# Down projection of a SwiGLU feed-forward network: newest hidden tiles taken from SBUF, residual loads spread over the steps, the second pass begun with a kept tile

## The chip, the cores and the metric

The kernel runs on one core of a Trainium2 chip. A core has five engines that work at the same time, each through its own queue of instructions in a fixed order: PE (matrix multiplications), DVE (elementwise vector work), ACT (activations and casts), POOL (elementwise work as well) and SP, which here issues DMAs. They wait for each other by semaphores. The metric is the device time of one execution in microseconds (us); lower is better.

## The reference, cut to what matters

Two layers are computed for 1024 tokens of 1024 numbers. Each ends with a feed-forward network behind a residual and a layer norm:

```python
def swiglu_ffn(x, w_in, w_out):
    gate, up = jnp.split(x @ w_in, 2, axis=-1)
    return (jax.nn.silu(gate) * up) @ w_out

for layer in range(2):
    ...
    x = _layer_norm(ALPHA * x + mix, ln_mix_g[layer], ln_mix_b[layer])
    x = _layer_norm(ALPHA * x + swiglu_ffn(x, ffn_w_in[layer], ffn_w_out[layer]),
                    ln_ffn_g[layer], ln_ffn_b[layer])
```

The hidden size is 2816. All is float32. The change concerns the product with `w_out`, called the down projection here, its residual `ALPHA * x`, and the norm behind it.

## The kernel before

`ffn` runs once per layer. Its first part, `hidden(j)` for 22 tiles j of 128 hidden numbers, makes a tile `hf` of h (128 hidden numbers by 1024 tokens): DVE writes its first half at L695 and its second at L699, from `u2` (L697) after ACT's Silu (L698), and SP stores it to memory (`scr_h`, L700), since all 22 tiles of h with their splits would not fit in SBUF.

The second part is the down projection, `down(0)` and `down(1)`: a pass for each half of the 1024 output numbers. A pass has 22 steps, one per hidden tile. A step needs two operands in two parts each, a high part cast by ACT (L197) and a low part subtracted by DVE (L200), both from `split`: the tile of h read back from memory (`load_hidden`: `wraw` to `hh` and `hl`, 128x1024) and a block of `f_out` (`block`: `wraw` to the two halves of `wb`, 128x512 each). `raw_load` has three buffers (`N_RAW = 3`), and a next load waits until a split has freed one. `mm3` (L229 to L231) makes three matmuls for each of eight token tiles: high by high, high by low, low by high. So a step is 24 matmuls, into eight PSUM banks `pd`, one per token tile.

At the end of a pass DVE adds the bank of each token tile to the residual, `acc = ALPHA * acc + pd` (L722), and takes statistics of it (L723). `acc` are eight tiles of 128x1024, loaded in step 0 of `down(0)` (L735, all eight one after the other) and multiplied and shifted by the gain of the norm before (`ln_gain`, two instructions of POOL each, L352 and L353, with `g_row` and `b_row`).

The last six tiles of h (`KEEP = 6`) stay split in SBUF from the first pass to the second. In `down(1)` the first sixteen steps run as above; then the six kept tiles run with the token tile as the outer loop, so that a token tile is finished early and its norm can follow: `ln` in layer 0, `ln_out` in layer 1, which writes the result (L754 to L769). `ln_out` needs the last norm's `g_row` and `b_row`. They are loaded between the two calls of `down`, into the same two buffers (tag `row`) that the rows of `ln_gain` hold.

The order on each engine's queue is set by a scheduler that goes by data dependences and estimates of its own; `pace` gives it one more dependence, on the last matmul written so far, which orders the instruction and makes nothing wait on the chip.

## Time and profile before

| | us |
|---|---|
| median of 3 runs | 2683.41 |
| lowest and highest run | 2683.39, 2695.26 |
| the profiled execution | 2686.94 |
| its span | 2685.1 |
| PE busy | 2533.1 (94%) |
| DVE busy | 1672.4 (62%) |
| ACT busy | 1135.9 (42%) |
| POOL busy | 505.3 (19%) |

The span is the part of the execution that the profiler recorded; starts in the rows count from its beginning. The down projection of layer 0 begins at 775.40 us, that of layer 1 at 2402.41 us. In a row of a timeline the bracket at the end tells how long the engine had stood idle before, and whose work released it. PE is busy nearly all the time, so what is looked for are the stretches in which it isn't.

### The profile page before, as it was taken

Reading aid. Unit: us, or ns where it says so; the run is one execution under the profiler, and the core shown is the slowest. Engines: PE = TensorE matmul, PEld = TensorE weight load, DVE = VectorE, ACT = ScalarE, POOL = GpSimd, SP = SyncE. Lnnn points to the kernel's source line nnn. Section 1 sums busy time; section 2 is a strip of 40 time slices with the busy share of each in tenths; the row PEclk is TensorE's granted clock in tenths of the full one; section 3 lists DMA queues with packets and bytes.
Section 4 is the critical chain, followed back from the end, with each engine's and each line's share of the span. In section 5 each row is a group of like instructions: output and inputs, shape, how many; then the busy total and the mean of one; then the engine's idle time right before and its main releaser. Section 6 shows DMA issues by size and latency. Waiting matters only on the chain. (4 is left out here: it accounts for less than half of the span.)

```text
span 2685.1 us, 41451 instructions
## 1 busy us (share of the span) xinstructions
PE 2533.1 (94%) x16064; PEld 2018.1 (75%) x16064; DVE 1672.4 (62%) x2981; ACT 1135.9 (42%) x2192; POOL 505.3 (19%) x526
## 2 busy tenths in 40 slices
...
GB/s 143 124 25 114 107 85 88 86 77 81 79 160 199 135 99 95 168 153 177 203 165 101 92 95 88 69 48 131 67 102 102 79 79 86 79 130 183 177 106 63
DMA packets 258181, 297.89 MB, mean 111 GB/s; under 512 B 149952, under 2 KB 191040, under 8 KB 257984
## 3 DMA queue, kind: packets, MB, share of 16 engines
...
## 5 line engine op out<-in xcount | busy, mean ns | idle before, releaser
L641 PE MATMUL py<-xch,wb 128*128 128x512 f32 x1056 | 356.6, 400 | 4.4 <-DVE u L690 2.4
L229 PE MATMUL pd<-wb,hh 128*128 128x512 f32 x704 | 282.2, 401 | 21.9 <-ACT wb L197 14.2
L197 ACT CAST wb<-wraw 128x512 fp32r<-128x512 f32 x220 | 135.2, 619 | 376.8 <-PE py L641 173.9
L231 PE MATMUL pd<-wb,hl 128*128 128x512 f32 x704 | 281.9, 400 | 6.9 <-DVE hl L200 6.9
L230 PE MATMUL pd<-wb,hh 128*128 128x512 f32 x704 | 281.4, 400 | 1.5 <-DVE wb L200 1.5
L200 DVE TENSOR_TENSOR wb<-wraw,wb 128x512 fp32r<-128x512 f32 x220 | 161.0, 735 | 145.1 <-ACT wb L197 143.0
L641 PEld LDWEIGHTS py<-xch,wb 128*128 128x128 f32 x1056 | 200.3, 190 | 62.8 <-DVE u L690 15.7
L641 PE MATMUL pz<-xch,wb 128*128 128x512 f32 x704 | 233.4, 393 | 4.5 <-ACT xch L197 4.5
L641 PE MATMUL px<-xch,wb 128*128 128x512 f32 x704 | 233.9, 395 | 3.2 <-ACT p L652 3.2
L352 POOL TENSOR_TENSOR acc<-acc,g_row 128x1024 f32<-128x1024 f32 x24 | 62.4, 2605 | 845.3 <-DMA acc<-res 824.0
L197 ACT CAST wb<-sums 128x512 fp32r<-128x512 f32 x176 | 108.6, 621 | 257.1 <-PE pz L641 144.3
L641 PE MATMUL py<-xcl,wb 128*128 128x512 f32 x528 | 209.4, 397 | 1.6 <-DVE xcl L200 1.6
L200 DVE TENSOR_TENSOR wb<-sums,wb 128x512 fp32r<-128x512 f32 x176 | 123.2, 703 | 102.3 <-ACT wb L197 101.5
L200 DVE TENSOR_TENSOR hl<-wraw,hh 128x1024 fp32r<-128x1024 f32 x76 | 107.1, 1411 | 115.8 <-ACT hh L197 115.8
L229 PEld LDWEIGHTS pd<-wb,hh 128*128 128x128 f32 x704 | 135.7, 193 | 55.7 <-ACT wb L197 15.5
L231 PEld LDWEIGHTS pd<-wb,hl 128*128 128x128 f32 x704 | 135.0, 192 | 38.2 <-DVE hl L200 7.8
L1180 PEld LDWEIGHTS <-lt 128*128 128x128 f16 x1792 | 88.5, 103 | 97.1 <-issue 71.3
L230 PEld LDWEIGHTS pd<-wb,hh 128*128 128x128 f32 x704 | 135.2, 192 | 33.4 <-DVE wb L200 2.7
L641 PEld LDWEIGHTS pz<-xch,wb 128*128 128x128 f32 x704 | 132.5, 189 | 34.5 <-ACT xch L197 5.3
L641 PEld LDWEIGHTS px<-xch,wb 128*128 128x128 f32 x704 | 131.9, 188 | 34.9 <-ACT p L652 5.5
L269 POOL TENSOR_TENSOR rstd<-ve,mhalf 128x1 f32<-128x1 f32 x48 | 37.9, 792 | 627.0 <-DVE ve L267 590.9
L1180 PE MATMUL pX<-lt 128*128 128x64 f16 x1280 | 92.3, 201 | 63.1 <-DVE lt L1313 33.4
...
## 6 DMA issues: line engine op xcount, KB each, us to landing
wraw<-in_f_in_dram SPq DMA_DIRECT2D x96, 512.0 KB, 3.6
wraw<-scr_h SPq DMA_DIRECT2D x76, 512.0 KB, 3.9
scr_h<-hf SPq DMA_DIRECT2D x44, 512.0 KB, 2.6
...
res<-acc SPq DMA_DIRECT2D x16, 512.0 KB, 2.6
acc<-res SPq DMA_DIRECT2D x16, 512.0 KB, 6.7
wraw<-in_w_r_dram SPq DMA_DIRECT2D x16, 512.0 KB, 3.8
wraw<-in_w_k_dram SPq DMA_DIRECT2D x16, 512.0 KB, 4.2
```

Source lines behind the costliest of these rows:

```text
L197: nc.scalar.copy(hi, src)
L200: return (eng or nc.vector).tensor_tensor(lo, src, f(hi), op=ALU.subtract)
L229: nc.tensor.matmul(ps, ls(ah), rs(bh), start=start, stop=False)
L230: nc.tensor.matmul(ps, ls(ah), rs(bl), start=False, stop=False)
L231: c.last_mm = nc.tensor.matmul(ps, ls(al), rs(bh), start=False, stop=stop)
L269: c.last_pow = nc.gpsimd.tensor_tensor(r, ve, c.mhalf[:, 0:1], op=ALU.pow)
L352: c.nc.gpsimd.tensor_tensor(x, x, rows[0], op=ALU.mult)
L641: c.last_mm = nc.tensor.matmul(ps, a_[:, k * P:(k + 1) * P], b_[:, k % 2, :], start=start and k == i == 0, stop=False, skip_group_check=True)
L1180: keep(nc.tensor.matmul(*a, **k))
```

## The change

Five things are changed in the down projection.

1. The tiles of h are taken in another order: 20, 21, then 0 to 19. The last two, just made, are split from `hf` in SBUF (`fresh`) instead of being read back. They are stored for the second pass a little later, when their step is loaded.
2. A step's weight block is loaded and split ahead of its tile of h.
3. The eight `acc` are loaded one per step, in steps 4 to 11 (`ACC_AT = 4`), not all in step 0.
4. The last norm's rows are loaded in step 13 of the first pass, by an entry that `pace` puts there, not between the passes.
5. The second pass begins with a kept tile (19), then reads 20, 21, 0 to 13, and ends with the five kept tiles 14 to 18 in the loop over token tiles. The steps at positions 1 and 2 are loaded in the middle of the step before, and the low half of their weight is put behind that place (`late`).

```diff
--- before.py
+++ after.py
@@ -67,6 +67,7 @@
 LN_A = {3: (0,), 4: (1,), 5: (2,), 6: (3,)}
 JP = 4
 KEEP = 6
+ACC_AT = 4
 BANKS = "bbbaaacc"
 HP = 4
 CH = 64
@@ -163,9 +164,11 @@
                        bufs=dict(a=NB_A, b=NB_B, c=NB_C)[which])
 
 
-def bcast_row(c, row_ap, n, name):
+def bcast_row(c, row_ap, n, name, late=False):
     t = c.pool.tile([P, 1024], F32, name=name, tag="row", bufs=2)
-    c.nc.sync.dma_start(t[:, 0:n], row_ap[:, 0:n].to_broadcast([P, n]))
+    d = c.nc.sync.dma_start(t[:, 0:n], row_ap[:, 0:n].to_broadcast([P, n]))
+    if late:
+        pace(c, d)
     return t
 
 
@@ -353,8 +356,8 @@
     c.nc.gpsimd.tensor_tensor(x, x, rows[1], op=ALU.add)
 
 
-def ln_rows(c, name):
-    return bcast_row(c, c.row(name + "_g"), D, "g_row"), bcast_row(c, c.row(name + "_b"), D, "b_row")
+def ln_rows(c, name, late=False):
+    return [bcast_row(c, c.row(name + e), D, e[1] + "_row", late) for e in ("_g", "_b")]
 
 
 
@@ -627,11 +630,13 @@
 
     nc = c.nc
 
-    def block(src):
+    def block(src, late=False):
 
         t_ = c.pool.tile([P, 1024], F32R, name="wb", tag="w", bufs=N_W)
         hi, lo = t_[:, 0:512], t_[:, 512:1024]
-        split(c, hi, lo, src)
+        last = split(c, hi, lo, src)
+        if late:
+            pace(c, last)
         return hi, lo
 
     def prod(ps, w, name, start=False):
@@ -697,12 +702,15 @@
         nc.vector.tensor_tensor(u2, pz, u2, op=ALU.add)
         nc.scalar.activation(u2, u2, AF.Silu)
         nc.vector.tensor_tensor(hf[:, 512:1024], u3, u2, op=ALU.mult)
-        nc.sync.dma_start(hscr[j], hf)
-
-    acc, dest, kept = [None] * 8, [], {}
+        if j < NHT - 2:
+            nc.sync.dma_start(hscr[j], hf)
+        else:
+            fresh[j] = hf
+
+    acc, dest, kept, fresh = [None] * 8, [], {}, {}
 
     def load_hidden(i):
-        raw = raw_load(c, hscr[i])
+        raw = fresh.pop(i) if i in fresh else raw_load(c, hscr[i])
         hi, lo = big(c, "hh", F32R), big(c, "hl", F32R)
         split(c, hi, lo, raw)
         return hi, lo
@@ -710,37 +718,54 @@
     def down(n):
         s = slice(n * 512, (n + 1) * 512)
         ps = [None] * 8
-        tail = list(range(NHT - KEEP, NHT))
-
-        def mm(tt, i, hs, w):
-            if i == 0:
+
+        order = [NHT - 2, NHT - 1] + list(range(NHT - 2))
+        keep_ = order[-KEEP:]
+        if n:
+            order = keep_[-1:] + order[:-KEEP] + keep_[:-1]
+        tail = order[-KEEP + 1:] if n else []
+
+        def mm(tt, at, hs, w):
+            if at == 0:
                 ps[tt] = bank(c, BANKS[tt], "pd")
-            mm3(c, ps[tt], hs, w, i == 0, i == NHT - 1, lambda y: y[:, tt * P:(tt + 1) * P], lambda w_: w_)
-            if i == NHT - 1:
+            mm3(c, ps[tt], hs, w, at == 0, at == NHT - 1, lambda y: y[:, tt * P:(tt + 1) * P], lambda w_: w_)
+            if at == NHT - 1:
                 if n == 0:
                     st[tt] = norm_stats(c, D)
                 nc.vector.scalar_tensor_tensor(acc[tt][:, s], acc[tt][:, s], ALPHA, ps[tt], op0=ALU.mult, op1=ALU.add)
                 nc.vector.bn_stats(st[tt][:, n, :], acc[tt][:, s])
 
-        def load(i):
+        def load(at, late=False):
+
+            i = order[at]
+            if n == 0 and i in fresh:
+                pace(c, nc.sync.dma_start(hscr[i], fresh[i]))
+            w = block(raw_load(c, f_out[layer, i][:, s], 512)[:, 0:512], late)
             hs = kept[i] if i in kept else load_hidden(i)
-            if n == 0 and i in tail:
+            if n == 0 and i in keep_:
                 kept[i] = hs
-            return hs, block(raw_load(c, f_out[layer, i][:, s], 512)[:, 0:512])
-        for i in range(NHT - KEEP if n else NHT):
-            hs, w = load(i)
-            if n == i == 0:
-                for tt in range(8):
-                    acc[tt] = big(c, "acc")
-                    nc.sync.dma_start(acc[tt], res[tt * P:(tt + 1) * P, :])
-                    ln_gain(c, acc[tt], rows_)
+            return hs, w
+        nxt = None
+        for at in range(NHT - len(tail)):
+            hs, w = nxt or load(at)
+            nxt = None
+            if n == 0 and 0 <= at - ACC_AT < 8:
+                tt = at - ACC_AT
+                acc[tt] = big(c, "acc")
+                pace(c, nc.sync.dma_start(acc[tt], res[tt * P:(tt + 1) * P, :]))
+                ln_gain(c, acc[tt], rows_)
+            if n == 0 and final is not None and at == ACC_AT + 9:
+                last_rows.extend(ln_rows(c, lnname, True))
             for tt in range(8):
-                mm(tt, i, hs, w)
+                mm(tt, at, hs, w)
+                if n and at < 2 and tt == 3:
+
+                    nxt = load(at + 1, True)
         if n:
-            ops = [load(i) for i in tail]
+            ops = [load(NHT - len(tail) + x) for x in range(len(tail))]
             for tt in range(8):
-                for i, (hs, w) in zip(tail, ops):
-                    mm(tt, i, hs, w)
+                for x, (hs, w) in enumerate(ops):
+                    mm(tt, NHT - len(tail) + x, hs, w)
                 if final is not None:
                     ln_out(tt)
                 elif tt > 1:
@@ -748,12 +773,13 @@
             if final is None:
                 ln(6)
                 ln(7)
-            
+    last_rows = []
     st = [None] * 8
 
     def ln_out(tt):
         a, rows_ = acc[tt], slice(tt * P, (tt + 1) * P)
         mean, r = norm(c, None, a, D, st[tt])
+        g_row, b_row = last_rows
         if tt < 7:
             nb = small(c, [P, 1], "nb", "nb")
             nc.vector.scalar_tensor_tensor(nb, mean, -1.0, r, op0=ALU.mult, op1=ALU.mult)
@@ -794,8 +820,6 @@
             aside()
     rows_ = ln_rows(c, before)
     down(0)
-    if final is not None:
-        g_row, b_row = ln_rows(c, lnname)
     down(1)
     return dest
```

The kernel's lines move by this: L197 and L200 become L200 and L203, L352 and L353 become L355 and L356, L697 becomes L702, L722 becomes L735, the load of `acc` becomes L755.

First place: DVE, layer 0, end of the last hidden tile (`hf_5714` before, `hf_5713` after; the last but one is `hf_5580` after). Before:

```order
L694 TENSOR_TENSOR up_5732<-py_5648,p1_5624 128x512
L695 TENSOR_TENSOR hf_5714<-up_5732,p1_5624 128x512
L200 TENSOR_TENSOR hl_5761<-wraw_5758,hh_5760 128x1024
L697 TENSOR_TENSOR u2_5697<-pz_5649,u2_5697 128x512
L699 TENSOR_TENSOR hf_5714<-u3_5665,u2_5697 128x512
L200 TENSOR_TENSOR hl_5836<-wraw_5833,hh_5835 128x1024
```

After:

```order
L699 TENSOR_TENSOR up_5731<-py_5647,p1_5623 128x512
L700 TENSOR_TENSOR hf_5713<-up_5731,p1_5623 128x512
L203 TENSOR_TENSOR hl_5763<-hf_5580,hh_5762 128x1024
L702 TENSOR_TENSOR u2_5696<-pz_5648,u2_5696 128x512
L704 TENSOR_TENSOR hf_5713<-u3_5664,u2_5696 128x512
L203 TENSOR_TENSOR hl_5805<-hf_5713,hh_5804 128x1024
```

The first `hl` is made from a tile of h in SBUF after and from one read back before; it stands at the same place, and the second `hl` is that of the last tile.

Second place: SP, layer 1, the loads of the first pass's early steps (`scr_h` is h, `in_f_out` the weight, `res1` the residual; in the rows after, `acc_22497` is the first of eight). Before:

```order
L735 DMA acc_22377<-res1_83 128x1024
L735 DMA acc_22381<-res1_83 128x1024
L735 DMA acc_22385<-res1_83 128x1024
L174 DMA wraw_22462<-in_f_out_dram 128x512
L174 DMA wraw_22491<-scr_h_84 128x1024
L174 DMA wraw_22497<-in_f_out_dram 128x512
L168 DMA g_row_23180<-in_rows_dram 128x1024
L174 DMA wraw_22526<-scr_h_84 128x1024
L168 DMA b_row_23182<-in_rows_dram 128x1024
L174 DMA wraw_22532<-in_f_out_dram 128x512
```

After:

```order
L177 DMA wraw_22603<-in_f_out_dram 128x512
L177 DMA wraw_22608<-scr_h_84 128x1024
L755 DMA acc_22497<-res1_83 128x1024
L177 DMA wraw_22642<-in_f_out_dram 128x512
L755 DMA acc_22536<-res1_83 128x1024
L177 DMA wraw_22647<-scr_h_84 128x1024
L177 DMA wraw_22681<-in_f_out_dram 128x512
L755 DMA acc_22575<-res1_83 128x1024
L177 DMA wraw_22686<-scr_h_84 128x1024
L177 DMA wraw_22720<-in_f_out_dram 128x512
```

Before, the eight loads of `acc` stand together, but for a store (three of them are shown), and `g_row` and `b_row` of the last norm right behind them among the loads of steps; after, each `acc` stands between a step's loads, and the rows of the norm come 27 places behind the first `acc`.

Third place: DVE, layer 0, the end of the first pass. The additions to `acc` are L722 before and L735 after. Before:

```order
L200 TENSOR_TENSOR hl_6778<-wraw_6775,hh_6777 128x1024
L200 TENSOR_TENSOR hl_6813<-wraw_6810,hh_6812 128x1024
L200 TENSOR_TENSOR wb_6783<-wraw_6781,wb_6783 128x512
L200 TENSOR_TENSOR wb_6818<-wraw_6816,wb_6818 128x512
L200 TENSOR_TENSOR wb_6853<-wraw_6851,wb_6853 128x512
L722 SCALAR_TENSOR_TENSOR acc_5769<-acc_5769,pd_5801 128x512
L722 SCALAR_TENSOR_TENSOR acc_5773<-acc_5773,pd_5805 128x512
```

After (the last `hl` of the first pass is `hl_6537`):

```order
L203 TENSOR_TENSOR hl_6537<-wraw_6534,hh_6536 128x1024
L203 TENSOR_TENSOR wb_6590<-wraw_6588,wb_6590 128x512
L203 TENSOR_TENSOR hl_6617<-wraw_6614,hh_6616 128x1024
L203 TENSOR_TENSOR hl_6656<-wraw_6653,hh_6655 128x1024
L203 TENSOR_TENSOR wb_6697<-wraw_6695,wb_6697 128x512
L203 TENSOR_TENSOR hl_6703<-wraw_6700,hh_6702 128x1024
L203 TENSOR_TENSOR wb_6732<-wraw_6730,wb_6732 128x512
L735 SCALAR_TENSOR_TENSOR acc_5913<-acc_5913,pd_5766 128x512
L735 SCALAR_TENSOR_TENSOR acc_5952<-acc_5952,pd_5770 128x512
```

And a little further on in the kernel after:

```order
L735 SCALAR_TENSOR_TENSOR acc_6147<-acc_6147,pd_5790 128x512
L735 SCALAR_TENSOR_TENSOR acc_6186<-acc_6186,pd_5794 128x512
L203 TENSOR_TENSOR wb_6611<-wraw_6609,wb_6611 128x512
L203 TENSOR_TENSOR hl_6738<-wraw_6735,hh_6737 128x1024
L203 TENSOR_TENSOR wb_6767<-wraw_6765,wb_6767 128x512
L203 TENSOR_TENSOR wb_6650<-wraw_6648,wb_6650 128x512
```

After, the first pass's last `hl` is followed by splits of the second pass, and the low halves `wb_6611` and `wb_6650` of its steps 1 and 2 stand behind all eight additions, with their loads made before.

## Rows read from the trace of the kernel before

**Rows 1.** Page, part 1: busy us (share of span), instructions of each engine.

```profile
PE 2533.1 (94%) x16064; PEld 2018.1 (75%) x16064; DVE 1672.4 (62%) x2981; ACT 1135.9 (42%) x2192; POOL 505.3 (19%) x526
```

**Rows 2.** Windows, PE, tile pd: window, us, busy (instructions), granted clock, DMA share, GB/s.

```profile
920.00:940.00 20.00, 20.00 (x88) 1.00 0.34 119
```

**Rows 3.** Timeline, PE, layer 0: start, duration, instruction, [idle before, and its releaser].

```profile
775.40 0.39 PE L229 MATMUL pd<-wb,hh 128*128 128x512 f32 x1
...
779.55 0.51 PE L231 MATMUL pd<-wb,hl 128*128 128x512 f32 x1 [3.52 <-DVE hl L200]
...
914.04 0.77 PE L229 MATMUL pd<-wb,hh 128*128 128x512 f32 x1 [5.08 <-DVE acc L722]
```

**Rows 4.** Timeline, PE, layer 1's first pass and its end.

```profile
2402.41 0.39 PE L229 MATMUL pd<-wb,hh 128*128 128x512 f32 x1
...
2445.71 0.79 PE L229 MATMUL pd<-wb,hh 128*128 128x512 f32 x1 [10.66 <-ACT wb L197]
...
2548.96 0.48 PE L229 MATMUL pd<-wb,hh 128*128 128x512 f32 x1 [1.08 <-DVE acc L722]
```

**Rows 5.** Timeline, SP (issues of DMAs), layer 1's first pass.

```profile
2413.73 0.51 SPq L174 DMA_DIRECT2D wraw<-in_f_out_dram  x1
2435.39 0.33 SPq L168 DMA_DIRECT2D g_row<-in_rows_dram  x1
```

**Rows 6.** Waits, SP, 2380 to 2686: waiter, waited for, us, times, longest.

```profile
SPq L168 <- POOL acc L352: 20.9, 1, 20.9
```

**Rows 7.** Waits, PE, 2550 to 2686 (layer 1's second pass).

```profile
PE pd L229 <- DVE acc L722: 1.4, 2, 0.7
```

**Rows 8.** Timeline, DVE, layer 0: the first hl.

```profile
776.14 3.36 DVE L200 TENSOR_TENSOR hl<-wraw,hh 128x1024 fp32r<-128x1024 f32 x1
```

**Rows 9.** Timeline, DVE, layer 0: stretch without POOL, first and last of 14 hl.

```profile
823.34 1.23 DVE L200 TENSOR_TENSOR hl<-wraw,hh 128x1024 fp32r<-128x1024 f32 x1 [0.89 <-ACT hh L197]
...
871.71 1.23 DVE L200 TENSOR_TENSOR hl<-wraw,hh 128x1024 fp32r<-128x1024 f32 x1 [1.92 <-ACT hh L197]
```

**Rows 10.** Instructions reading g_row: count: ns min/median/max, first and last start.

```profile
L352 POOL TENSOR_TENSOR acc<-acc,g_row x24: 2342/2406/3427, 766.0 to 2433.0; 128x1024 f32<-128x1024 f32 x24
```

**Rows 11.** Timeline, DVE, layer 0: splits of two steps while POOL works on acc.

```profile
799.14 2.87 DVE L200 TENSOR_TENSOR wb<-wraw,wb 128x512 fp32r<-128x512 f32 x1
...
811.44 2.89 DVE L200 TENSOR_TENSOR wb<-wraw,wb 128x512 fp32r<-128x512 f32 x1
```

**Rows 12.** Timeline, DVE, layer 0: last split and first additions at the passes' boundary.

```profile
912.61 0.69 DVE L200 TENSOR_TENSOR wb<-wraw,wb 128x512 fp32r<-128x512 f32 x1 [3.93 <-ACT wb L197]
913.22 1.28 DVE L722 SCALAR_TENSOR_TENSOR acc<-acc,pd 128x512 f32<-128x512 f32 x2
```

**Rows 13.** Page, part 6: DMA issues, count, KB each, median us to landing.

```profile
acc<-res SPq DMA_DIRECT2D x16, 512.0 KB, 6.7
```

**Rows 14.** Timeline, SP, layer 0: issues ahead of the boundary.

```profile
893.45 0.32 SPq L174 DMA_DIRECT2D wraw<-scr_h  x1
...
899.00 0.32 SPq L174 DMA_DIRECT2D wraw<-scr_h  x1
...
904.71 0.33 SPq L174 DMA_DIRECT2D wraw<-in_f_out_dram  x1
...
908.71 0.32 SPq L174 DMA_DIRECT2D wraw<-scr_h  x1
```

**Rows 15.** Windows, PE, tile pd, the step behind layer 0's boundary.

```profile
914.04:922.05 8.01, 7.85 (x26) 0.80 0.11 34
```

**Rows 16.** Groups, DVE, L722 in 2630:2686, then 1005:1050: busy, mean ns | idle before.

```profile
L722 DVE SCALAR_TENSOR_TENSOR acc<-acc,pd 128x512 f32<-128x512 f32 x8 | 5.5, 681 | 19.2 <-PE pd L231 19.2
...
L722 DVE SCALAR_TENSOR_TENSOR acc<-acc,pd 128x512 f32<-128x512 f32 x8 | 5.5, 686 | 7.4 <-PE pd L231 7.4
```

**Rows 17.** Windows, all engines: us, busy, then clock, DMA share, GB/s.

```profile
800.00:820.00 20.00, 20.00 (x86) 16.26 (x85) 19.34 (x8) 5.07 (x7) 16.51 (x6) 0.97 0.40 135
820.00:840.00 20.00, 20.00 (x88) 16.31 (x87) 9.43 (x11) 8.88 (x11) 0.00 (x0) 1.00 0.67 221
```

## The prediction

> **What bounds the kernel now.** I read the profile's busy shares first, then the matmuls of `pd` on PE, then what the late ones waited for, then that waiter's own queue. PE is busy for 94% of the span [rows 1], so outside its idle stretches a change can only move work that PE doesn't see. In the middle of a pass of the down projection, 88 matmuls take 20.00 us at a granted clock of 1.00 [rows 2]: 0.2273 us each. A step (one hidden tile, eight token tiles, three matmuls each) is 24 of them, 5.455 us, and a pass of 22 steps is 120.0 us.
>
> The first pass takes longer than that. From the first matmul of `pd` to the first of the second pass it is 914.04 − 775.40 = 138.64 us in layer 0 [rows 3] and 2548.96 − 2402.41 = 146.55 us in layer 1 [rows 4]. So 18.6 and 26.5 us are lost, and the rows say where: 3.52 us at the third matmul, on `hl`, the low half of the first tile of h; 5.08 us at the boundary of the passes, on the DVE addition to `acc` (L722), with slow matmuls behind it; in layer 1, 10.66 us on a weight, `wb`. That last wait begins in SP's queue: after the weight issued at 2413.73 the next entry is `g_row` at 2435.39 [rows 5], and SP stood 20.9 us before it, waiting for the POOL multiplication of the last `acc` [rows 6]. Behind it in the queue stood the next loads of h and of weights. In layer 1's second pass the list of PE's waits holds nothing but 1.4 us on that addition [rows 7].
>
> **Parts that remove something.** *Start.* Before, the first `hl` comes from a tile read back from memory, runs 3.36 us on DVE from 776.14 [rows 8], and PE stands 3.52 us. After, tile 20's split reads `hf` in SBUF, which was complete one hidden tile earlier; its `hl` is queued behind the last tile's L700 and ahead of L702. POOL has no `acc` to work on at that time, so I price it at 1.23 us, the `hl` of a quiet stretch [rows 9], done near 775.6, before the third matmul needs it. The last tile's own `hl` then ends near 780.2, and step 1 starts at 780.85. So the start costs 0 to 0.3 us. The two stores of h move behind those splits; nobody reads them before the second pass.
>
> *Loads of acc.* Before, all eight stand in SP's queue around step 2. After, one stands between two weights, from step 7's loads on. What is not removed is POOL's work: two instructions of a median 2.406 us [rows 10] for each of eight tiles. Before, with POOL on them, DVE goes from one `wb` at 799.14 to the second next at 811.44 [rows 11]: 6.15 us for a step's two splits (`wb`, `hl`), against PE's 5.455. In a quiet stretch 13 steps take 871.71 − 823.34 [rows 9], 3.72 each. What the new load adds to a contended step no row shows. Lower bound 6.14, the row. The upper bound is everything one after another, 2 × 2.406 + 1.23 + 0.69 [rows 9, 10, 12] = 6.73. I take 6.4, between them, since the new queue puts an `acc` load (6.7 us to landing [rows 13]) ahead of each next load, where the rows of before had theirs behind them.
>
> The Trainium skill (SBUF — State Buffer, "Who interferes with whom") says that a DVE instruction with two SBUF inputs contends with a GpSimd instruction that reads SBUF. It calls the shared port pair an exclusive lock. By that the 6.73 would hold, and the sum below would be −30.1 us. The trace agrees in kind (`hl` in 3.36 us against 1.23), and its 6.15 is under 6.73.
>
> *Where DVE is, then.* Let S be the first matmul of `pd`. The `hl` of step 1 ends at S+4.8, those of steps 2 to 4, whose loads already lie in the three raw slots, 1.23 each later, S+8.5. A slot turns over in 4.0 us with a weight (904.71 to 908.71) and 5.55 with a tile of h (893.45 to 899.00) [rows 14]. Two weights and one h in line, and three short splits ahead on DVE (3.15), bring `hl` of step 7 to S+8.5+8.0+5.55+3.15 = S+25.2. Eight contended steps (7 to 15): 8 × 6.4 = 51.2. Six quiet ones: 22.3. So `hl` of step 21, the last, is done at S+98.7, 16 us before PE reaches its step. PE therefore never waits inside the pass: at step 15 DVE stands at S+76.4, PE needs it at S+81.8.
>
> *Final rows.* In layer 1 they move to step 13 of the pass, where POOL ends its last `acc` by about the same time; a wait of SP there is at most some 2 us, with 5 us of lead. So the 20.9 us of SP and PE's 10.66 go.
>
> **Parts that add something.** *Boundary.* Two weights of the second pass's steps 1 and 2 have their low half split late, behind the eight L735 additions on DVE. Until then each holds one of three raw slots. So the loads ahead of the first L735 go through one slot, one by one: h, h, w, h, w in layer 0, 3 × 5.6 + 2 × 4.0 = 24.8 us; h, h, w, h in layer 1, 20.8 us. DVE reaches its first L735 at S+98.7+24.8 = S+123.5 in layer 0 and S+119.5 in layer 1. Before, PE's first matmul of the second pass starts 0.8 us behind that addition (913.22 [rows 12], 914.04 [rows 3]). PE itself is done at S+120.3. Boundary: S+124.25 and, by PE, S+120.3. That is 138.64 − 124.25 = **14.4 us** less in layer 0 and 146.55 − 120.3 = **26.2 us** less in layer 1. The step behind the boundary is paced by the same eight additions as before (8.01 us for 26 matmuls, [rows 15]) and stays.
>
> *Tail.* The second pass begins with a kept tile, and five tiles instead of six are left for the loop over token tiles. The first token tile then ends later by 7 × 3 × 0.2273 = 4.8 us against PE's end. In layer 1 DVE's normalization waits for PE once, 19.2 us before the first tile, then never [rows 16]; its chain sets the end of the kernel, so **+4.8 us**. In layer 0 eight tiles share 7.4 us of such waits [rows 16], of which 4.6 lie behind the first; they take up the shift. I put **+0.5**, between 0 and 2.
>
> **Sum.** −14.4 − 26.2 + 4.8 + 0.5 = −35.3 us. The profiled execution took 2686.94 us: 2651.6. The median of the runs, 2683.41, is 0.9987 of it: **2648 us**. With 6.14 a step it is 2646 (layer 1 is at PE's bound already), with 6.73 it is 2653.
>
> **The rivals.**
>
> *The contended steps are strictly serial* (6.73 a step): 2653. For: the long `hl` [rows 8]. Against: 6.15 [rows 11].
>
> *Supply falls behind.* A step's loads (512 KB of h, 256 KB of weight, 512 KB of `acc`) per 5.455 us are 240 GB/s. From 800 to 820, with POOL at work, 135 GB/s moved, and 221 GB/s from 820 to 840 [rows 17]. If the latency of an `acc` load in front of each weight makes a step 7.5, DVE is 8.8 us later per layer: boundary S+133.05 and S+129.05, sum −17.8, 2666.
>
> *Slower than before.* The same place and mechanism: one price, the contended step. With P for it, the sum is −35.3 + 16 × (P − 6.4) once both layers are DVE's; zero lies near 8.6 us, half a per cent slower (13.4 us, about what a measurement of this kernel can tell from no change) near 9.4. At 10 us the time is 2706. For: `acc` landed in 6.7 us, so a queue that let one load wait for the other could reach it. Against: SP only issues, and DMA engines were 0.40 busy from 800 to 820 [rows 17].
>
> *The start isn't cleared.* If `hl` of tile 20 still takes 3.4 us ahead of L702, up to 3.5 us per layer come back: 2655. Against: POOL is idle there.
>
> *Better.* If the late blocks cost nothing and both boundaries are PE's, with a step of 5.455 behind them (1.9 us less than 8.01 × 24/26 = 7.39), the sum is −18.3 − 26.2 − 3.8 + 4.8 = −43.5: 2640.
>
> **How the numbers follow.** Forecast 0.45, strictly serial 0.20, supply behind 0.15 (2658 to 2676), better 0.10, start 0.05, slower 0.04; 0.01 for no change at all. The range 2638 to 2668 leaves out the upper half of "supply behind", slower and part of "better", under 2 in 10. Below 2670 counts as faster: 0.90; within half a per cent 0.06; slower 0.04.
>
> **What would show it.** Right: no PE wait on `hl` at the third matmul of `pd`; no SP wait on POOL for `g_row` beyond 2 us and no `wb` wait in layer 1's first pass; `hl` 6.1 to 6.7 us apart while POOL works; in layer 0 a wait of PE on the addition to `acc` at the boundary, near S+124; the DVE chain at the end 4.8 us later behind PE's last matmul. Wrong: waits of PE on `wb` or `hl` between steps 5 and 16 (supply), a boundary later than S+130, or a layer 0 tail that grows by over 2 us. The first number to fall would be the contended step, which is the least sure.

## The result, and the profile after

The changed kernel takes 2653.05 us (median of four runs, 2651.39 to 2657.45), the kernel before 2688.69 (four runs, with those shown above, 2683.39 to 2695.26). The ratio is 0.988, with a 95% interval of 0.9857 to 0.9902: about 32 us less. The forecast was 2648 in a range of 2638 to 2668.

The page of the changed kernel has PE busy for 15 us less than [rows 1], and a load of `acc` lands in 4.2 us where [rows 13] has 6.7:

```profile
PE 2517.7 (95%) x16064; PEld 2004.7 (75%) x16064; DVE 1697.4 (64%) x2981; ACT 1136.5 (43%) x2192; POOL 517.8 (19%) x526
...
acc<-res SPq DMA_DIRECT2D x16, 512.0 KB, 4.2
```

Its matmuls of `pd` at the places of [rows 3] and [rows 4] (start, duration, instruction, idle before and releaser; layer 0, then layer 1):

```profile
775.11 0.39 PE L232 MATMUL pd<-wb,hh 128*128 128x512 f32 x1
...
775.57 0.39 PE L234 MATMUL pd<-wb,hl 128*128 128x512 f32 x1
...
898.97 0.63 PE L232 MATMUL pd<-wb,hh 128*128 128x512 f32 x1 [1.95 <-DVE acc L735]
...
2390.47 0.39 PE L232 MATMUL pd<-wb,hh 128*128 128x512 f32 x1
...
2514.31 0.48 PE L232 MATMUL pd<-wb,hh 128*128 128x512 f32 x1 [1.69 <-DVE acc L735]
```

The third matmul follows at once; in the kernel before it waited 3.52 us. There is no wait on a weight in layer 1. What is left is one wait at each boundary of the passes, 1.95 and 1.69 us (in layer 1 with two short ones behind it, 1.3 us together). The windows of the two first passes, first matmul to first matmul of the second pass, with their granted clock (window, us, busy, clock, DMA share, GB/s):

```profile
775.11:898.97 123.86, 121.91 (x528) 1.00 0.51 170
2390.47:2514.31 123.84, 122.16 (x528) 1.00 0.53 176
```

So the span, 2685.1 before and 2655.7 after, is split like this. Each stretch is the difference of two starts in the two timelines.

| stretch | before | after | difference | forecast |
|---|---|---|---|---|
| start to first `pd`, layer 0 | 775.40 | 775.11 | −0.3 | 0 |
| first pass, layer 0 | 138.64 | 123.86 | −14.8 | −14.4 |
| second pass, layer 0, to the next stage's first matmul | 128.84 | 128.10 | −0.7 | +0.5 |
| from there to the first `pd` of layer 1 | 1359.5 | 1363.4 | +3.9 | 0 |
| first pass, layer 1 | 146.55 | 123.84 | −22.7 | −26.2 |
| second pass, layer 1, to the end | 136.2 | 141.4 | +5.2 | +4.8 |

The 3.9 us in the middle are in work whose order the change leaves alone. In the profiled executions of the experiments below the same stretch took from 1353 to 1367 us, so they are put down to the execution, not to the change.

A first pass ends with the later of two things: PE's last matmul, its waits included, and DVE's first addition to `acc`. In layer 0 PE was done 133.6 us after its first matmul before and is done after 121.9 now (the start of the second pass less the idle time ahead of it). DVE's addition came at 137.8 [rows 12] and comes at 123.0. In layer 1 PE was done at 145.5 and is at 122.2, and the addition came at 145.7 and comes at 123.0. So DVE sets the end in all four, in layer 1 before only just. DVE's last split of the pass has hardly moved: in layer 0 it ended 97.5 us after the first matmul before [rows 9] and ends at 97.9 now, in layer 1 105.9 and 102.3. What shrank is the stretch from there to the addition. Before, sixteen splits stood in it in either layer, 40.3 and 39.8 us; now there are six in layer 0, 25.2 us, and five in layer 1, 20.8. So PE's waits had to go, but the length of the pass follows DVE's queue. DVE in layer 1 of the kernel before, the last `hl` of the pass and the first addition:

```profile
2507.12 1.22 DVE L200 TENSOR_TENSOR hl<-wraw,hh 128x1024 fp32r<-128x1024 f32 x1 [2.27 <-ACT hh L197]
...
2548.13 1.28 DVE L722 SCALAR_TENSOR_TENSOR acc<-acc,pd 128x512 f32<-128x512 f32 x2
```

DVE in layer 0 of the kernel after, at the places of [rows 8], [rows 11], [rows 9] and [rows 12]: the first `hl`, two `hl` while POOL works on `acc`, the last `hl` of the first pass, and all splits from there to the first addition:

```profile
773.92 1.22 DVE L203 TENSOR_TENSOR hl<-hf,hh 128x1024 fp32r<-128x1024 f32 x1
...
809.60 3.42 DVE L203 TENSOR_TENSOR hl<-wraw,hh 128x1024 fp32r<-128x1024 f32 x1
...
815.75 3.43 DVE L203 TENSOR_TENSOR hl<-wraw,hh 128x1024 fp32r<-128x1024 f32 x1
...
871.74 1.23 DVE L203 TENSOR_TENSOR hl<-wraw,hh 128x1024 fp32r<-128x1024 f32 x1 [0.88 <-ACT hh L200]
873.02 0.69 DVE L203 TENSOR_TENSOR wb<-wraw,wb 128x512 fp32r<-128x512 f32 x1
877.48 1.23 DVE L203 TENSOR_TENSOR hl<-wraw,hh 128x1024 fp32r<-128x1024 f32 x1 [3.77 <-ACT hh L200]
883.40 1.23 DVE L203 TENSOR_TENSOR hl<-wraw,hh 128x1024 fp32r<-128x1024 f32 x1 [4.70 <-ACT hh L200]
887.89 0.69 DVE L203 TENSOR_TENSOR wb<-wraw,wb 128x512 fp32r<-128x512 f32 x1 [3.27 <-ACT wb L200]
892.96 1.23 DVE L203 TENSOR_TENSOR hl<-wraw,hh 128x1024 fp32r<-128x1024 f32 x1 [4.37 <-ACT hh L200]
897.53 0.69 DVE L203 TENSOR_TENSOR wb<-wraw,wb 128x512 fp32r<-128x512 f32 x1 [3.35 <-ACT wb L200]
898.14 1.28 DVE L735 SCALAR_TENSOR_TENSOR acc<-acc,pd 128x512 f32<-128x512 f32 x2
```

The first `hl` takes 1.22 us and is done before the first matmul. With POOL at work a step's two splits take 815.75 − 809.60 = 6.15 us. The last split of the pass ends at 872.97, 97.9 us after the first matmul. Behind it stands a `wb` whose load was already there, then five splits whose loads went one at a time. The addition that PE waits for starts at 898.14, 25.2 us behind the last split.

In layer 1 the last split comes later. SP, ACT and DVE there (the rows' loads at step 13, the load of h behind them, its cast, the last `hl`, the first addition):

```profile
2466.13 0.42 SPq L169 DMA_DIRECT2D g_row<-in_rows_dram  x1
2466.65 0.38 SPq L169 DMA_DIRECT2D b_row<-in_rows_dram  x1
2467.36 0.33 SPq L177 DMA_DIRECT2D wraw<-scr_h  x1
...
2475.57 1.05 ACT L200 CAST hh<-wraw 128x1024 fp32r<-128x1024 f32 x1 [5.63 <-DMA wraw<-scr_h]
...
2491.50 1.23 DVE L203 TENSOR_TENSOR hl<-wraw,hh 128x1024 fp32r<-128x1024 f32 x1 [0.95 <-ACT hh L200]
...
2513.49 1.28 DVE L735 SCALAR_TENSOR_TENSOR acc<-acc,pd 128x512 f32<-128x512 f32 x2
```

The load of h issued at 2467.36 is there at 2475.57, 8.2 us later. SP waited for nobody at the rows. The last split ends at 2492.73, 102.3 us after the first matmul, and the addition starts 20.8 us later.

The additions of layer 1's second pass (the group of [rows 16]):

```profile
L735 DVE SCALAR_TENSOR_TENSOR acc<-acc,pd 128x512 f32<-128x512 f32 x8 | 5.4, 681 | 24.3 <-PE pd L234 24.3
```

DVE still waits for PE once, 24.3 us and not 19.2, and its chain sets the end.

### The profile page after: what moved, and what is told of

It reads as the page before. It is cut to its first block, busy times and chain, and to the rows that moved or that the text cites. A ratio compares the mean times of both kernels' runs of the same rounds, so it can differ in the third digit from the quotient of the medians.

```text
span 2655.7 us, 41419 instructions
## 1 busy us (share of the span) xinstructions
PE 2517.7 (95%) x16064; PEld 2004.7 (75%) x16064; DVE 1697.4 (64%) x2981; ACT 1136.5 (43%) x2192; POOL 517.8 (19%) x526
## 3 DMA queue, kind: packets, MB, share of 16 engines
q1 hardware_dynamic: 256256, 291.05, 35.3%
## 4 chain that ended last, share of the span: by engine, by line
PE 65%; DVE 9%; issue 9%; DMA 7%; POOL 6%; ACT 4%; SPq 1%; DVEq 0%; ACTq 0%; POOLq 0%
PE py L646 14%; PE pz L646 9%; PE px L646 8%; DMA wraw<-in_f_out_dram 2%; PE pv L232 2%; PE pd L232 1%; PE pd L233 1%; PE pd L234 1%; PE po L232 1%; PE po L233 1%; PE po L234 1%; PE pv L233 1%; POOL acc L355 1%; PE pv L234 1%; PE pA L1204 1%
## 5 line engine op out<-in xcount | busy, mean ns | idle before, releaser
L200 ACT CAST wb<-wraw 128x512 fp32r<-128x512 f32 x220 | 135.6, 619 | 398.6 <-PE py L646 177.4
L232 PE MATMUL pd<-wb,hh 128*128 128x512 f32 x704 | 277.5, 394 | 5.1 <-DVE acc L735 5.0
L233 PE MATMUL pd<-wb,hh 128*128 128x512 f32 x704 | 277.7, 394 | 0.0
L203 DVE TENSOR_TENSOR wb<-wraw,wb 128x512 fp32r<-128x512 f32 x220 | 171.8, 784 | 112.9 <-ACT wb L200 110.6
L355 POOL TENSOR_TENSOR acc<-acc,g_row 128x1024 f32<-128x1024 f32 x24 | 65.8, 2743 | 897.6 <-DMA acc<-res 880.3
L200 ACT CAST wb<-sums 128x512 fp32r<-128x512 f32 x176 | 108.8, 622 | 256.7 <-PE pz L646 145.2
L203 DVE TENSOR_TENSOR wb<-sums,wb 128x512 fp32r<-128x512 f32 x176 | 123.0, 702 | 102.6 <-ACT wb L200 101.7
L203 DVE TENSOR_TENSOR hl<-wraw,hh 128x1024 fp32r<-128x1024 f32 x72 | 126.9, 1771 | 89.5 <-ACT hh L200 89.4
L193 DVE TENSOR_TENSOR wlo<-wraw,whi 128x1024 fp32r<-128x1024 f32 x82 | 103.0, 1262 | 69.9 <-ACT whi L192 46.8
```

Of the source, the lines that this page charges most:

```text
L193: (lo_eng or nc.vector).tensor_tensor(lo, raw, f(hi), op=ALU.subtract)
L200: nc.scalar.copy(hi, src)
L203: return (eng or nc.vector).tensor_tensor(lo, src, f(hi), op=ALU.subtract)
L232: nc.tensor.matmul(ps, ls(ah), rs(bh), start=start, stop=False)
L233: nc.tensor.matmul(ps, ls(ah), rs(bl), start=False, stop=False)
L355: c.nc.gpsimd.tensor_tensor(x, x, rows[0], op=ALU.mult)
```

## The experiments

The first pass of a layer, below, is the time from its first matmul of `pd` to that of the second pass; the waits are those of PE in it. Whole times are medians, and the ratio of each is to runs of the kernel before on the same chip. The kernels ran on different chips, so two of them are compared by their ratios.

| kernel | whole, us | ratio to before (95%) | first pass, layers 0 and 1 | wait at the start | wait at the boundary |
|---|---|---|---|---|---|
| before | | | 138.6, 146.6 | 3.5, 3.4 | 5.1, 1.1 |
| after | 2653.1 | 0.988 (0.9857 to 0.9902) | 123.9, 123.8 | 0, 0 | 2.0, 1.7 |
| start_undone | 2662.9 | 0.9906 (0.9878 to 0.9933) | 127.3, 125.3 | 0, 0 | 5.1, 2.7 |
| acc_together | 2678.4 | 0.997 (0.9956 to 0.9985) | 135.7, 136.3 | 3.3, 2.8 | 9.0, 9.7 |
| second_pass_as_before | 2656.5 | 0.9875 (0.9843 to 0.9907) | 126.6, 129.2 | 0, 0 | 4.7, 7.2 |
| start_alone | 2684.4 | 0.9992 (0.9977 to 1.0007) | 140.5, 144.9 | 3.4, 3.2 | 13.6, 4.6 |
| spread_alone | 2664.9 | 0.9928 (0.9914 to 0.9942) | 130.0, 130.6 | 0, 0 | 7.7, 8.5 |
| rows_in_second_pass | 2655.2 | 0.9879 (0.9863 to 0.9896) | 124.3, 124.2 | 0, 0 | 2.4, 2.1 |
| no_gain | 2647.9 | 0.9849 (0.983 to 0.9867) | 121.8, 122.0 | 0, 0 | 0, 0 |
| no_late | 2657.5 | 0.989 (0.987 to 0.991) | 126.4, 124.7 | 0, 0 | 4.5, 2.6 |
| late_weights_unsplit | 2645.5 | 0.985 (0.9828 to 0.9872) | 121.8, 122.0 | 0, 0 | 0, 0 |
| together_unsplit | 2652.4 | 0.9883 (0.9865 to 0.9902) | 126.7, 126.3 | 3.4, 2.7 | 0, 0 |
| start_undone_unsplit | 2645.6 | 0.9863 (0.9844 to 0.9882) | 121.9, 122.2 | 0, 0 | 0, 0 |
| unsplit_eight_kept | 2631.4 | 0.9806 (0.9789 to 0.9823) | 121.8, 122.3 | 0, 0 | 0, 0 |

Where PE waits for nothing, the first pass is PE's own 121.8 to 122.3 us. That is more than the 120.0 of the prediction and of the expectations below. A window of 20 us lists 88 matmuls [rows 2], but the ones cut by its edges are among them, and only 86 start in it; from start to start there they are 0.2303 us each, and 528 in 121.7 us are 0.2305, not 0.2273. So where an expectation has 120.3 to 121 us for a pass that PE sets, 121.8 to 122.3 is that case.

### What removed the wait at the start

**start_undone**, the tiles of h in the order 0 to 21 and from memory:

```diff
-        order = [NHT - 2, NHT - 1] + list(range(NHT - 2))
+        order = list(range(NHT))
...
-        if j < NHT - 2:
-            nc.sync.dma_start(hscr[j], hf)
-        else:
-            fresh[j] = hf
+        nc.sync.dma_start(hscr[j], hf)
```

> The changed kernel with one part undone: the tiles of h are taken in the order 0 to 21 again and all are read back from memory; nothing is split from SBUF. In the changed kernel the first pass takes 123.9 us in layer 0 and 123.8 in layer 1, from its first matmul to the first of the second pass. Theory (the start costs PE its wait, and DVE the longer first split): the wait of PE on the first low half of h is back with 2 to 3.5 us in each layer, DVE is 2 to 4 us later, and the first pass takes 126 to 127.5 us in both; the whole 4 to 8 us over the changed kernel's 2653, so 2657 to 2661. Rival (the wait at the boundary of the passes, which DVE sets, takes up what is lost at the start): the first pass stays within 1 us of 124, the whole within 2 us of 2653.

The whole grew by more than the theory has it (2662.9 against 2657 to 2661), and not where it has it: PE does not wait at the start at all. The first `hl`, from a tile read back, takes 1.22 us on DVE. The loss stands at the boundary: POOL begins on `acc` 25.9 us after the first matmul, not 22.1, and DVE's last split of the pass ends at 101.5, not 97.9, with 25.0 us from there to the addition, where the changed kernel has 25.2. The first `hl`, the last one of the pass and PE at the boundary:

```profile
775.11 1.22 DVE L203 TENSOR_TENSOR hl<-wraw,hh 128x1024 fp32r<-128x1024 f32 x1
...
876.53 1.23 DVE L203 TENSOR_TENSOR hl<-wraw,hh 128x1024 fp32r<-128x1024 f32 x1 [1.68 <-ACT hh L200]
...
903.61 0.76 PE L232 MATMUL pd<-wb,hh 128*128 128x512 f32 x1 [5.10 <-DVE acc L732]
```

**start_alone** puts only this part on the kernel before:

```diff
-        tail = list(range(NHT - KEEP, NHT))
+        order = [NHT - 2, NHT - 1] + list(range(NHT - 2))
+        tail = order[-KEEP:]
...
-        raw = raw_load(c, hscr[i])
+        raw = fresh.pop(i) if i in fresh else raw_load(c, hscr[i])
```

> The kernel before with one part of the change: the tiles of h in the order 20, 21, 0 to 19, the first two split from SBUF. Theory: PE's 3.5 us at the first low half go in both layers. The first pass of layer 0, 138.6 us before, ends when DVE is ready for the additions and shrinks by 1 to 3.5; that of layer 1, 146.6 before, keeps its 10 us wait on a weight, since the norm's rows still stand in the queue, and shrinks by 2 to 4. The whole 3 to 8 us under the kernel before. Rival (the start is hidden behind the later waits): both within 1 us of before, the whole within 2 us of it.

The ratio's interval holds 1, as the rival has it, but again for another reason: the wait at the start isn't hidden, it is still there. The split now reads `hf` in SBUF and takes 3.36 us as before:

```profile
775.69 3.36 DVE L200 TENSOR_TENSOR hl<-hf,hh 128x1024 fp32r<-128x1024 f32 x1
...
779.11 0.50 PE L231 MATMUL pd<-wb,hl 128*128 128x512 f32 x1 [3.38 <-DVE hl L200]
```

The first pass of layer 0 would not have been shorter without that wait: PE is done 126.9 us after its first matmul (140.5 less 13.6), and DVE's addition comes at 139.7. The wait on a weight in layer 1 is still there with 8.9 us, as the theory has it.

**spread_alone** puts only the spreading of the residual loads on the kernel before:

```diff
-            if n == i == 0:
-                for tt in range(8):
-                    acc[tt] = big(c, "acc")
-                    nc.sync.dma_start(acc[tt], res[tt * P:(tt + 1) * P, :])
-                    ln_gain(c, acc[tt], rows_)
+            if n == 0 and 0 <= i - ACC_AT < 8:
+                tt = i - ACC_AT
+                acc[tt] = big(c, "acc")
+                pace(c, nc.sync.dma_start(acc[tt], res[tt * P:(tt + 1) * P, :]))
+                ln_gain(c, acc[tt], rows_)
```

> The kernel before with one part of the change: the residual tiles are loaded one per step in steps 4 to 11; order of the tiles, reading back, rows and second pass stay as before. Theory (PE's 3.4 us at the first low half of h come from POOL, which works on the residual at that time, and need no tile in SBUF; the norm's rows now find POOL done): the wait at the start is gone in both layers, the 10.7 us on a weight in layer 1 are gone, the first pass takes 124 to 130 us in both layers, ended by the splits of the second pass that stand ahead of the first addition; the whole 20 to 32 us under the kernel before. Rival (the start needs the tile in SBUF): 3.4 us at the first low half stay in both layers, and the whole comes down by less than 20.

The waits at the start and on the weight are gone, with every tile read back from memory. What PE still waits for in the down projection of layer 0 is one row of its list (waiter, waited for, us, times, longest), the additions at the boundary:

```profile
PE pd L230 <- DVE acc L723: 10.8, 2, 7.7
```

The whole came down by 18 us, less than forecast, since the boundary lies at 130 us, the far end of what was expected. So one part, the spreading, clears the start in both layers and the 10.7 us of layer 1. Yet PE, done 122.3 us after its first matmul in layer 0, waits for DVE, and there the gain comes from the stretch ahead of the addition. DVE's last split ends 101.7 us after the first matmul, later than the 97.5 of the kernel before. The addition follows after 27.5 us and not 40.3, with fifteen splits between:

```profile
875.40 1.23 DVE L201 TENSOR_TENSOR hl<-wraw,hh 128x1024 fp32r<-128x1024 f32 x1 [1.51 <-ACT hh L198]
...
904.14 0.68 DVE L723 SCALAR_TENSOR_TENSOR acc<-acc,pd 128x512 f32<-128x512 f32 x1
```

A step of two splits takes about 5.5 us in that stretch of the kernel before and 3.9 here. The scheduler orders the queues anew with each edit, and which of their differences makes this one was not tested.

### What the loads of acc cost when they stand together

**acc_together**:

```diff
-            if n == 0 and 0 <= at - ACC_AT < 8:
-                tt = at - ACC_AT
-                acc[tt] = big(c, "acc")
-                pace(c, nc.sync.dma_start(acc[tt], res[tt * P:(tt + 1) * P, :]))
-                ln_gain(c, acc[tt], rows_)
+            if n == at == 0:
+                for tt in range(8):
+                    acc[tt] = big(c, "acc")
+                    nc.sync.dma_start(acc[tt], res[tt * P:(tt + 1) * P, :])
+                    ln_gain(c, acc[tt], rows_)
```

> The changed kernel with one part undone: all eight residual tiles are loaded in step 0 again, one after the other; the last norm's rows stay at step 13. Theory (in layer 1 the 20.9 us of SP came from the rows' place behind the eight loads, not from the eight loads themselves): a wait of PE on a weight of 1 to 4 us early in the pass comes back, as in layer 0 before, POOL's work ends earlier in the pass, and the first pass takes 122 to 128 us in both layers; the whole within 5 us of 2653. Rival (spreading the loads is what cleared the queue): the first pass of layer 1 is back at 135 us or more, and the whole at 2664 or more.

The rival's numbers came, and the theory's part on this is wrong. But the queue isn't the cause either: PE waits on no weight. It waits at the start, where the `hl` from SBUF runs beside POOL's first two instructions and takes 3.35 us, and 8.97 us at the boundary (POOL, DVE, PE in turn):

```profile
773.69 2.41 POOL L355 TENSOR_TENSOR acc<-acc,g_row 128x1024 f32<-128x1024 f32 x1 [399.83 <-DMA acc<-res]
776.18 2.66 POOL L356 TENSOR_TENSOR acc<-acc,b_row 128x1024 f32<-128x1024 f32 x1
...
776.57 3.35 DVE L203 TENSOR_TENSOR hl<-hf,hh 128x1024 fp32r<-128x1024 f32 x1
...
779.98 0.51 PE L234 MATMUL pd<-wb,hl 128*128 128x512 f32 x1 [3.26 <-DVE hl L203]
...
911.77 0.77 PE L232 MATMUL pd<-wb,hh 128*128 128x512 f32 x1 [8.97 <-DVE acc L735]
```

Between the last split of the first pass and the first addition DVE has, behind the `wb` already loaded, seven splits here, not five, with loads one at a time:

```profile
873.61 1.22 DVE L203 TENSOR_TENSOR hl<-wraw,hh 128x1024 fp32r<-128x1024 f32 x1 [3.93 <-ACT hh L200]
...
880.38 1.23 DVE L203 TENSOR_TENSOR hl<-wraw,hh 128x1024 fp32r<-128x1024 f32 x1 [4.35 <-ACT hh L200]
...
905.75 1.23 DVE L203 TENSOR_TENSOR hl<-wraw,hh 128x1024 fp32r<-128x1024 f32 x1 [4.43 <-ACT hh L200]
...
910.94 1.28 DVE L735 SCALAR_TENSOR_TENSOR acc<-acc,pd 128x512 f32<-128x512 f32 x2
```

(The last `hl` of the pass is shown, then the first and the last of the four `hl` among the seven; two more and three `wb` are left out.) The last split of the pass ends at 874.83, 98.7 us after the first matmul, within 1 us of the changed kernel; the seven then take 36 us.

**together_unsplit** tells the two shares apart. It is acc_together with the edit of late_weights_unsplit (below), which puts those splits behind the additions.

> The changed kernel with the residual loaded together in step 0, as in acc_together, and with the splits of the late weights' steps behind the additions, as in late_weights_unsplit. In acc_together the first pass took 135.7 and 136.3 us, 3 of them at the start and 9 and 9.7 at the boundary. Theory (the boundary's share comes from seven loads, one at a time, between the last split of the first pass and the first addition, and not from the loads of acc): the boundary's wait is gone in both layers, the start's 3 us stay, the first pass takes 123 to 125 us; the whole 2647 to 2654. Rival (the loads of acc themselves starve the pass): the first pass stays at 130 us or more.

The boundary's wait is gone in both layers, and the start's stays, as the theory has it; the whole is in its range. The first pass, 126.7 and 126.3 us, is over it by 1.5: PE's own pass is longer than was assumed, and behind the wait, in which PE stood 3.4 us, matmuls start up to 0.43 us apart for a while. The granted clock is 0.56 from 778.8 to 782.6 in layer 0, so mostly the lower of its two levels (1.2 GHz), and 1.00 from 785 on. In layer 0 the one wait of PE in the whole down projection:

```profile
PE pd L236 <- DVE hl L205: 3.4, 1, 3.4
```

### What sets the boundary

**second_pass_as_before**, tile 20 first and six kept tiles at the end:

```diff
-            order = keep_[-1:] + order[:-KEEP] + keep_[:-1]
-        tail = order[-KEEP + 1:] if n else []
+            order = order[:-KEEP] + keep_
+        tail = order[-KEEP:] if n else []
...
-                if n and at < 2 and tt == 3:
-                    nxt = load(at + 1, True)
```

> The changed kernel with one part undone: the second pass begins with tile 20, read back, and ends with six kept tiles in the loop over token tiles; no weight is put late. Theory: the splits that stand ahead of the first addition to acc grow to seven steps' worth, some 26 us behind the last split of the first pass at 3.72 a step, against 25.2 and 21 now; the first pass takes 123 to 128 us in both layers; at the end the norm begins 4.8 us earlier against PE's last matmul, so from the second pass to the end of the span layer 1 takes 136.5 us and not 141.4. The whole 2645 to 2653. Rival (beginning with the kept tile is what shortened the boundary): the first pass takes 132 us or more in both layers, the whole 2660 or more.

The boundary came 2.7 and 5.4 us later (layer 1 by 1 us over what was expected), the end 5 us earlier against it (2663.2 − 2526.88 = 136.3), and the whole 3.5 us over the upper end of the forecast; the intervals of this kernel and the changed one overlap. PE at the two boundaries, and then the group of the additions of layer 1's second pass:

```profile
901.65 0.76 PE L232 MATMUL pd<-wb,hh 128*128 128x512 f32 x1 [4.67 <-DVE acc L735]
...
2526.88 0.77 PE L232 MATMUL pd<-wb,hh 128*128 128x512 f32 x1 [7.23 <-DVE acc L735]
```

```profile
L735 DVE SCALAR_TENSOR_TENSOR acc<-acc,pd 128x512 f32<-128x512 f32 x8 | 5.5, 682 | 19.4 <-PE pd L234 19.4
```

**no_late** leaves the two weights' splits where they were loaded:

```diff
-                    nxt = load(at + 1, True)
+                    nxt = load(at + 1)
```

> The changed kernel without putting the two weights late: their splits stand where they were loaded, and 14 splits of the second pass stand ahead of the first addition to acc, not five. Theory (the price of the boundary is the loads one at a time, as two of three raw slots are held): with three slots free these 14 splits take about 3.7 us a step, 5.5 steps or 20 to 22 us, and the first pass takes 119.5 to 123 us, no longer than now. Rival (the price is the number of splits ahead of the addition): the first pass takes 128 us or more in both layers and the whole 2661 or more.

The first pass took 126.4 and 124.7 us, a little over the theory's range and under the rival's. In layer 0 DVE has 14 splits of the second pass ahead of the first addition, seven of each kind, at the quiet rate: 26.5 us from the last split of the first pass. In layer 1 there are 13, in 23.5 us. I had counted five and a half steps, and it is seven, 7 × 3.72 = 26. So five splits with loads one at a time and fourteen with three slots cost about the same.

**rows_in_second_pass**:

```diff
-            if n == 0 and final is not None and at == ACC_AT + 9:
+            if n == 1 and final is not None and at == 4:
```

> The changed kernel, with the last norm's rows loaded in step 4 of the second pass, not in step 13 of the first. In the changed kernel the first pass of layer 1 takes 123.8 us; a load of h issued right behind the two rows landed some 8 us after its issue. Theory (the rows' own transfers delay that load, and all behind it, by some 4 us): DVE's last split of the first pass is 3.5 to 4.5 us earlier, and the first pass of layer 1 ends when PE is done, at 120.3 to 121 us; layer 0 stays at 123.9; the whole 2 to 4 us under 2653. Rival (the delay is the wait of SP or of DVE with POOL, not the rows): the first pass of layer 1 stays within 1 us of 123.8.

Half of the theory came. Without the rows the last split of the first pass in layer 1 ends at 2485.89, 98.6 us after the first matmul, 3.6 earlier than in the changed kernel. But the boundary stays, as the rival has it:

```profile
2484.66 1.23 DVE L203 TENSOR_TENSOR hl<-wraw,hh 128x1024 fp32r<-128x1024 f32 x1 [2.09 <-ACT hh L200]
...
2510.05 0.69 DVE L203 TENSOR_TENSOR wb<-wraw,wb 128x512 fp32r<-128x512 f32 x1 [3.64 <-ACT wb L200]
2510.66 1.28 DVE L735 SCALAR_TENSOR_TENSOR acc<-acc,pd 128x512 f32<-128x512 f32 x2
```

The order on DVE changed with the edit: behind the `wb` already loaded, five splits stand ahead of the first addition in layer 1 where four stood, the last a `wb` at 2510.05. They take 24.8 us and give back what the rows had cost.

**late_weights_unsplit** paces the load of the two late weights to the same place as their split:

```diff
-            w = block(raw_load(c, f_out[layer, i][:, s], 512)[:, 0:512], late)
+            raw = raw_load(c, f_out[layer, i][:, s], 512, late)
+            w = block(raw[:, 0:512], late)
...
+    if late:
+        pace(c, d)
     return raw
```

> The changed kernel, with the load of the two late weights paced to the same place as the low half of their split. On DVE the first additions to acc then stand right behind the last split of the first pass and that of one weight, and the splits of the second pass's steps 1 and 2 behind them. Theory (at the boundary PE waits for DVE because five loads, one at a time, stand ahead of the first addition): that wait is gone in both layers, the first pass takes 120.3 to 121 us in both, and the step behind it 5.5 to 6.5 us, not over 7; the whole 8 to 12 us under 2653, so 2641 to 2645. Rival (the splits that now come behind the additions starve steps 1 and 2 instead): the boundary is PE's, but waits of 3 us or more on a split follow in steps 1 to 3 of the second pass, and the whole stays within 4 us of 2653.

Only one `wb` now stands between the last split of the pass and the first addition, where DVE waits 19.0 us for PE. PE's list of waits is empty for the down projections of both layers, and the first passes are solid, 528 matmuls that fill their windows (these end just short of the second pass). DVE's first addition:

```profile
892.47 1.37 DVE L737 SCALAR_TENSOR_TENSOR acc<-acc,pd 128x512 f32<-128x512 f32 x2 [19.00 <-PE pd L236]
```

and the windows:

```profile
775.21:896.90 121.69, 121.69 (x528) 1.00 0.49 160
2383.03:2504.90 121.87, 121.87 (x528) 1.00 0.51 169
```

From the second pass's first matmul to the end layer 1 takes 139.3 us and not 141.4, since the step behind the boundary is no longer paced by the additions. The whole is 2645.5, 7.5 us under the changed kernel by the medians. The intervals of the two ratios overlap; the profiled executions show where the time goes, 2.1 and 1.9 us of the first passes and some 2 of each second pass. The wait at the boundary is thus set by what stands ahead of the first addition in DVE's queue.

**no_gain** leaves out POOL's multiplication and shift of the residual (`ln_gain`), so what it computes is another residual:

```diff
-                ln_gain(c, acc[tt], rows_)
```

> The changed kernel without POOL's multiplication and shift of the eight residual tiles (they are left out, so the residual is not the reference's); their loads stay. Theory (POOL's work makes a step's two splits 6.15 us, not 3.7): the low halves of h of steps 8 to 15 come 3.7 to 5.5 us apart, the last split of the first pass is done 15 us or more earlier than at S+98 and S+102, and the first pass ends with PE, 120.3 to 121 us in both layers; the whole 5 to 9 us under 2653. Rival (the loads of acc, not POOL, make the steps long): steps 8 to 15 stay at 5.8 us or more, and the first pass at 123 us or more.

In steps 8 to 15, where POOL worked before, the `hl` come 2.6 to 5.6 us apart, 4.2 in the mean, and the last split of the pass ends at 862.24, 85.6 us after the first matmul: 12.3 us earlier, not the 15 that were expected. DVE reaches the first addition with 6.5 us to spare:

```profile
813.42 1.23 DVE L203 TENSOR_TENSOR hl<-wraw,hh 128x1024 fp32r<-128x1024 f32 x1 [0.26 <-ACT hh L200]
...
818.79 1.23 DVE L203 TENSOR_TENSOR hl<-wraw,hh 128x1024 fp32r<-128x1024 f32 x1 [0.26 <-ACT hh L200]
...
861.01 1.23 DVE L203 TENSOR_TENSOR hl<-wraw,hh 128x1024 fp32r<-128x1024 f32 x1 [0.87 <-ACT hh L200]
...
893.79 1.37 DVE L735 SCALAR_TENSOR_TENSOR acc<-acc,pd 128x512 f32<-128x512 f32 x2 [6.52 <-PE pd L234]
```

So POOL's work beside DVE is what makes DVE late, and the splits ahead of the addition are what makes that lateness PE's. Either of them taken away, PE sets the boundary.

### A version that beats both

**start_undone_unsplit** is late_weights_unsplit without the tiles in SBUF.

> As late_weights_unsplit, with the tiles of h in the order 0 to 21 and all read back from memory. Theory (with POOL idle at the start the first low half is ready in time from memory too, and what start_undone lost was at the boundary): no wait of PE at the start, the first pass takes 120.3 to 121.5 us in both layers, the whole within 3 us of late_weights_unsplit's 2645.5. Rival (the tiles in SBUF save work of their own): the first pass, or the hidden phase ahead of it, is 1.5 us or more longer in each layer, and the whole 4 us or more over 2645.5.

2645.6 us here and 2645.5 there, no wait in either: as the theory has it. Once the boundary is PE's, the tiles from SBUF bring nothing that these runs can tell.

**unsplit_eight_kept** is late_weights_unsplit with eight kept tiles:

```diff
-KEEP = 6
+KEEP = 8
```

> As late_weights_unsplit, with eight kept tiles, so seven in the loop over token tiles at the end and one that begins the second pass. Theory (each tile of that loop lets the first token tile finish 7 x 3 x 0.2273 = 4.77 us earlier against PE's end, as DVE's chain sets the end of the kernel): from the first matmul of the second pass to the end of the span layer 1 takes some 9.5 us less than in late_weights_unsplit, and the whole 8 to 10 us less than its 2645.5, so 2635 to 2638. Rival (the room that 16 buffers of kept tiles take delays the loads): waits of PE on splits of 3 us or more in the second half of the first pass or in the second pass, and a gain under 4 us.

PE waits for nothing in layer 1's down projection. From the first matmul of the second pass to the end of the span it takes 130.5 us, where late_weights_unsplit takes 139.3: 8.8 us less, against 9.5 expected. The whole is 2631.4 us, 3.6 under the forecast, and 0.9806 of the kernel before (0.9789 to 0.9823), the fastest of these kernels. Its distance to start_undone_unsplit, on the same chip, is 14 us by the medians and 9 in the profiled executions; the loop at the end accounts for the 9, and the other 5 are open.

## Why the prediction was right, and where it was not

**The waits that go.** That the waits of PE at the start and on layer 1's weight would go was right, and for the 10.7 us the reason too: SP is no longer held at the rows [rows 5, 6], for POOL is done by then. The list left out one wait of the kernel before, 2.7 us on a weight in layer 0, which went with them. For the start the reason was half wrong. The step gave two causes for a short first `hl` that is early enough, the tile in SBUF and an idle POOL. start_alone and acc_together have the tile in SBUF and POOL at work: 3.36 and 3.35 us, and PE waits. start_undone and spread_alone have it from memory and POOL idle: 1.22 us, and PE doesn't wait. So it was POOL alone, and the term belongs to the spreading of the residual loads.

**Where the sum takes its time from.** The prediction books the start and the loads of `acc` under what is removed, and the boundary under what is added. The times are right, for it worked out when DVE reaches the addition and took the old pass as measured. But the rows give another split: in layer 0 the last split of the pass stayed where it was (97.5 and 97.9 us), and all of the 14.8 us come from the boundary, 40.3 us before and 25.2 after. In layer 1 3.7 us come from an earlier last split and 19.0 from the boundary. The prediction never read that stretch in the kernel before.

**The contended step.** I took 6.4 us between 6.14 and 6.73; it measures 6.15, the row of the kernel before [rows 11]. The load of `acc` ahead of each next load did not lengthen it. By the Trainium skill's rule (SBUF — State Buffer, "Who interferes with whom") the two engines would take turns wholly, 6.73; the trace agrees that the two hold each other up (`hl` 1.23 us alone, 3.42 beside POOL), and not in the sum. Two errors met here. `hl` of step 7 ended 31.7 us after the first matmul, not 25.2. Some 4 us of that are there because POOL was already at work when steps 6 and 7 were split (their two `hl` took 6.68 us, not 2 × 1.23); the rest lies ahead of them, where DVE waited for loads. From there to step 15 it took 42.7 us, not 51.2, since POOL was done by S+71. The last split of the pass came at S+97.9 where I had S+98.7; that the two errors nearly cancel is luck.

**The boundary in layer 0.** Five loads one by one: 24.8 forecast, 25.2 measured, with the addition at S+123.0 and PE's matmul at S+123.9 (forecast 123.5 and 124.25). Both steps of that working held, and DVE set this boundary, so the length of PE's own pass didn't matter.

**The boundary in layer 1.** This is the term that was mis-sized, 26.2 us forecast and 22.7 measured. The stretch from the last split to the addition was right, 20.8 us in both. The size was off for two reasons. "PE itself is done at S+120.3" was short: its own pass is 121.8 to 122.3 us, as the kernels without a wait show, because the 0.2273 us of a matmul was read from a window with cut edges. And "a wait of SP there is at most some 2 us" looked at the wrong thing: SP did not wait. The transfers of the two rows delayed the load of h behind them, which took 8.2 us to its cast, and through the slots all that followed. rows_in_second_pass shows the size, 3.6 us at the last split. With it DVE, and not PE, set layer 1's boundary, at S+123.8. Without it PE would have set it at about S+122.0, so of the 3.5 us by which the term was off, some 1.7 are PE's own pass and 1.8 the rows.

**The sum.** The profiled execution took 2657.45 us where the sum gave 2651.6. Of these 5.8 us 3.5 are the term of layer 1, 3.9 the middle that nobody touched, and the others together about −1.5. That the two medians of the result lie 35.6 us apart, nearly the 35.3 of the sum, is luck: the kernel before has a median of 2688.69 there and 2683.41 in the prediction, and the profiled spans lie 29.4 us apart.

**The tail.** +4.8 forecast, +5.2 measured in layer 1, with the one wait of DVE on PE grown by 5.1 us as it should (24.3 against 19.2). second_pass_as_before, with six tiles there, is back at 136.3. In layer 0 it cost nothing (−0.7; I had put +0.5).

**The rivals.** Supply did not fall behind: PE had no wait inside either pass, POOL at work or not. The slower case, which needed a step of 9.4 us, was far. The better case, 2640, with both boundaries PE's, is what late_weights_unsplit became, at 2645.5, with a pass of 121.8 and 122.0 us and not 120.3.

**What stays open.** start_undone's median is 9.8 us over the changed kernel's. In its profiled execution the two first passes account for 4.9 of that (3.4 and 1.5) and the hidden phase ahead of the first for 1.2; the intervals of the two overlap, and the rest was not followed further. No run undoes by itself the second part of the change, the weight loaded ahead of its tile of h, so what it brings is not shown. And since the scheduler orders the queues anew for each kernel, undoing one part can move others, as in rows_in_second_pass; the differences between two kernels are those of all that moved.
